# Scores of several heads in one PSUM bank, with one maximum and one mask, in a two-block transformer kernel

## The chip, the cores and the metric

The kernel runs on one core of one Trainium2 chip. Its metric is device time in microseconds for one execution, median of the runs. TensorE (PE) multiplies matrices into PSUM, whose eight banks hold 512 fp32 columns each; VectorE (DVE), ScalarE (ACT) and GpSimd (POOL) work element by element, GpSimd on SBUF alone; SyncE (SP) issues the DMA transfers. Each engine takes its instructions in the order in which they were laid down and waits on semaphores of the others.

## The reference

512 tokens of width 1024 pass two blocks in fp32: a gated linear attention layer, a sparse attention layer (four key heads with four query heads each, head width 64) and two hybrid layers (differential attention with four heads of two score maps each, beside stick-breaking attention with eight heads), each followed by a feed-forward network. What the change touches are two softmaxes.

In the sparse layer, with 512 tokens, all eight key blocks are selected, so the selected and the windowed attention are both plain causal softmaxes over the same queries:

```python
p_sel = masked_softmax(jnp.einsum('bkgqd,bkqmd->bkgqm', qc, ks) * scale, kpos <= qpos[:, None])
p_win = masked_softmax(jnp.einsum('bkgqd,bknd->bkgqn', qc, kw) * scale, win_mask)
o = gates[0] * o_cmp + gates[1] * o_sel + gates[2] * o_win
```

In the hybrid layers the weights are a difference of two softmaxes:

```python
sc = jnp.einsum('bhqd,bhkd->bhqk', qb, k).astype(jnp.float32) * scale
sc = jnp.where(mask, sc, -jnp.inf)
w = probs(qb1, k1) - lam * probs(qb2, k2)
```

## The kernel before, in words

Every fp32 value that goes into a large matmul is split into a high part of reduced precision (fp32r) and the rest, and a product is three matmuls (`mm3`, lines 321 to 323: high by high, low by high, high by low). Weights come as tiles of 128x1024 from memory, are split on ACT (L197) and DVE (L198), and feed the projections. These projections are most of PE's work.

The sparse layer (`nsa`) goes by head groups kh = 0 to 3 (one key head, four query heads), query blocks t of 128 tokens, and j = 0 (selected) or 1 (windowed): 32 units (kh, t, j). Groups 0 to 2 go through t = 0, 1, 2, 3, the last through 3, 2, 1, 0. A unit has two halves. `weights` takes, for each of four heads, n = (t+1)*128 columns of scores: two matmuls (L852, L853; keys high and low, the stacked query `qst` as the stationary operand) and a third that adds the causal mask from a bf16 identity and a 128x128 mask to the diagonal block (L854), all into a PSUM bank of the tag `pa`, of which there are three. Then DVE takes the negated row maximum (L1057), ACT the exponential with the row sum (L1059) into a tile of the tag `pe` (12 of them); after the four heads DVE makes the factors (reciprocal L1061, gate L1063) and scales the first head (L1069), POOL the three others (L1066). `values` transposes the weights on PE (L867, four heads' 128x128 blocks into one bank `pt`), splits them (ACT L870, DVE L871) and multiplies by the values into `po` (L1085, L1086); for j = 0 the compressed attention's weights go first (`ce`, L1079, L1080). `pipeline` calls `weights` of a unit ahead of `values` of the unit before.

The differential attention (`dweights1`, `dvalues`) does the same for four heads hd and two score maps c, with scores by `pair_scores` (L841 to L843), maximum L1275, exponential L1277, then reciprocal (L1279), the factor lambda (L1280), ACT's scaling of the second map (L1281) and DVE's combination (L1282). `dprep` prepares the next head's queries and keys: a rotation on POOL with a swapped copy by DMA, casts on ACT (L812, L824) and rests on DVE (L813, L825). The stick-breaking attention (`sweights1`) uses `pair_scores` too.

The order on each engine is not written out by hand: a scheduler of the tile framework lays all instructions down from its own estimate of times, tile by tile, with the buffer counts as limits. Functions of `fill` and `held` give it projections to lay between the units.

Of the kernel before, what the change touches and what calls it, by code (L numbers as in the profile page):

```python
# [17 lines left out]
AF = mybir.ActivationFunctionType  # L18
OP = mybir.AluOpType
AX = mybir.AxisListType  # L20

P = 128
# [75 lines left out]
class Kern:  # L98
# [10 lines left out]
    def setup(self, dram):  # L109
# [37 lines left out]
        for t, n in zip(bf, ("ident", "caus", "strict")):  # L147
# [7 lines left out]
                qst=8, sth=2, stl=2, q2h=2, q2l=2, k2h=4, k2l=4, pe=12, pth=4, ptl=4, otmp=1, on=4, onh=6, onl=6,  # L155
# [676 lines left out]
            out.append((k, lo))  # L832
        return out

    def pair_scores(self, q, k, t, mask):

        nc = self.nc
        n = (t + 1) * P
        ps = self.psum("pa")
        ts = slice(t * P, n)  # L840
        nc.tensor.matmul(ps[:, :n], q[:, ts], k[0][:, :n], start=True, stop=False)  # L841
        nc.tensor.matmul(ps[:, :n], q[:, ts], k[1][:, :n], start=False, stop=False)
        nc.tensor.matmul(ps[:, ts], self.identb, mask, start=False, stop=True)  # L843
        return ps[:, :n]

    def scores(self, q, k, t, mask):

        nc = self.nc
        n = (t + 1) * P
        ps = self.psum("pa")  # L850
        ts = slice(t * P, n)
        nc.tensor.matmul(ps[:, :n], q[:, ts], k[0][:, :n], start=True, stop=False)  # L852
        nc.tensor.matmul(ps[:, :n], q[:, ts], k[1][:, :n], start=False, stop=False)  # L853
        self.mask_mm = nc.tensor.matmul(ps[:, ts], self.identb, mask, start=False, stop=True)  # L854
        return ps[:, :n]

    def small(self, name, n, bufs=4, dt=F):
        if n > 16:
# [51 lines left out]
    def nsa(self, x):  # L910
        nc = self.nc
# [16 lines left out]
        for nb in range(2):  # L928
            nc.tensor.matmul(pk[:, :W], w2[:, nb * P:(nb + 1) * P], hid[:, nb * W:(nb + 1) * W],
                             start=nb == 0, stop=nb == 1)  # L930
# [38 lines left out]
        ps = self.psum("pd")  # L969
# [21 lines left out]
        def queries(kh, n):  # L991

            q = self.raw_block("nsa_w_in", 0, h, (2 * kh + n) * P, 0.125, "qs")
            st["q", kh, n] = q, self.stack_q(self.rope(q, tabs, eng=nc.vector))
# [42 lines left out]
        def weights(kh, t, j):  # L1037
            u = order[kh].index(t) * 2 + j
            if u == 0:
                if kh == 0:  # L1040
                    queries(0, 0)
                    queries(0, 1)
                    head_group(0)
                if kh < 3:
                    fill[:0] = [partial(queries, kh + 1, 0), partial(queries, kh + 1, 1), partial(head_group, kh + 1)]
            for i in range(pieces[kh][u]):
                if fill:
                    fill.pop(0)()
            qst, kd, o, e4 = st[kh]
            n = (t + 1) * P  # L1050
            sm = self.small("ss", 4)
            ps4 = []
            for g in range(4):
                sc = self.scores(qst[g], kd[j], t, self.causb)
                st["last"] = self.mask_mm
                mx = self.small("sm", 1, 8)
                nc.vector.tensor_reduce(mx, sc, axis=AX.X, op=OP.max, negate=True)  # L1057
                e = self.g("pe")
                nc.scalar.activation(e[:, :n], sc, AF.Exp, bias=mx, accum_out=sm[:, g:g + 1])  # L1059
                ps4.append(e)  # L1060
            nc.vector.reciprocal(sm, sm)  # L1061
            c = (j + 1) * 16 + kh * 4
            nc.vector.tensor_tensor(sm, sm, gate[:, t, c:c + 4], op=OP.mult)  # L1063
            for g in range(4):
                if g:
                    nc.gpsimd.tensor_scalar(ps4[g][:, :n], ps4[g][:, :n], sm[:, g:g + 1], 1.0,  # L1066
                                            op0=OP.mult, op1=OP.mult)
                else:
                    nc.vector.tensor_scalar(ps4[g][:, :n], ps4[g][:, :n], sm[:, g:g + 1], None, op0=OP.mult)  # L1069
            return ps4  # L1070

        def values(kh, t, j, ps4):
            qst, kd, o, e4 = st[kh]
# [36 lines left out]
        def out(n, ks, held=False):  # L1110
# [6 lines left out]
            nc.vector.tensor_tensor(xs[n], ps, xs[n], op=OP.add)  # L1117

        self.pipeline([(kh, t, j) for kh in range(4) for t in order[kh] for j in range(2)], weights, values)
        while fill:  # L1120
            fill.pop(0)()
# [62 lines left out]
    def hyb(self, x, layer, first):  # L1184
        nc = self.nc
# [4 lines left out]
        if first:  # L1190
# [9 lines left out]
            ps = self.psum("pt")  # L1200
            self.tok_sums(self.sqsum(x, gs), ps)
            a = self.sp.tile([P, 4], F, tag="ms", name="ms", bufs=3)
# [26 lines left out]
        for t, ps in enumerate(self.proj_wide(W, layer, h, (1024, 1280))):  # L1229
            sc = ycol[:, t:t + 1]  # L1230
# [23 lines left out]
        def dweights(hd):  # L1254
            if hd == 0:
                dprep(0)
            es = self.blocks("pe")
            ws = [dweights1(hd, 0, es[0])]
            if hd < 3:
                dprep(hd + 1)  # L1260
            for t in range(1, 4):
                ws.append(dweights1(hd, t, es[t]))
                if t == 2 and hd > 1:
                    svals(hd - 2)
            return ws

        def dweights1(hd, t, e0):
            q, k = st[hd]
            n = (t + 1) * P
            sm = self.small("ds", 2)  # L1270
            es = []
            for c in range(2):
                sc = self.pair_scores(q[c], k[c], t, self.causb)
                mx = self.small("sm", 1, 8)
                nc.vector.tensor_reduce(mx, sc, axis=AX.X, op=OP.max, negate=True)  # L1275
                e = self.g("pe")[:, :n] if c else e0
                nc.scalar.activation(e, sc, AF.Exp, bias=mx, accum_out=sm[:, c:c + 1])  # L1277
                es.append(e)
            nc.vector.reciprocal(sm, sm)  # L1279
            nc.vector.tensor_tensor(sm[:, 1:2], sm[:, 1:2], self.lam[:, layer:layer + 1], op=OP.mult)  # L1280
            nc.scalar.activation(es[1], es[1], AF.Copy, scale=sm[:, 1:2])  # L1281
            nc.vector.scalar_tensor_tensor(es[0], es[0], sm[:, 0:1], es[1], op0=OP.mult, op1=OP.subtract)  # L1282
            return es[0]
# [36 lines left out]
        def sweights(pr, a):  # L1320
            if a == 0 and pr == 0:
                sprep(0)
            rs = self.blocks("sbr")
            ws = [sweights1(pr, a, 0, rs[0])]
            if a == 0 and pr < 3:
                sprep(pr + 1)
            return ws + [sweights1(pr, a, t, rs[t]) for t in range(1, 4)]

        def sweights1(pr, a, t, r):
            q, k, o = st["s", pr]  # L1330
            n = (t + 1) * P
            z = self.pair_scores(q[a], k[a], t, self.strictb)
            l = self.g("sbl")[:, :n]
            nc.scalar.activation(l, z, AF.Abs)
            nc.scalar.activation(l, l, AF.Exp, scale=-1.0)
            nc.scalar.activation(l, l, AF.Ln, bias=1.0)
            nc.vector.scalar_tensor_tensor(l, z, 0.0, l, op0=OP.max, op1=OP.add)
            nc.vector.tensor_tensor_scan(r[:, ::-1], self.ones.to_broadcast([P, n]), l[:, ::-1], 0.0,
                                         op0=OP.mult, op1=OP.add)
            nc.vector.tensor_tensor(r, z, r, op=OP.subtract)  # L1340
            st["exp"] = nc.scalar.activation(r, r, AF.Exp)
            return r
# [22 lines left out]
        for n in range(16):  # L1365
            ps = self.proj(W, layer, h, 3072 + n * P)
            t = self.g("gate")
            nc.vector.tensor_tensor(t, ps, rbc, op=OP.mult)  # L1368
            gt.append(t)
        for n in range(16):  # L1370
            ins = nc.scalar.activation(gt[n], gt[n], AF.Sigmoid, bias=self.v("b_gate_2", layer, n))
            self.after(ins, last_exp)
        mh, ml = [], []
        for n in range(KB):
# [5 lines left out]
            a, b = self.split(gt[n], "mm")  # L1380
            mh.append(a)
            ml.append(b)
        for n in range(KB):
            ps = self.proj("w_out_2", layer, (mh, ml), n * P)
# [93 lines left out]
```

## Time and profile before

| | |
|---|---|
| median of 3 runs | 2833.21 us (2833.19 to 2834.01) |
| the profiled execution | 2835.08 us, of which the span of the trace is 2833.1 us |
| mean granted clock of TensorE | 0.991 |
| busy PE, DVE, ACT, POOL | 2773.4, 2019.9, 1366.3, 614.2 us |
| instructions | 39540, of them 14760 matmul records on PE |

The busy share is a mean over stages. The sparse layer's attention lies from 736 to 950 us, the differential attention from 1393 us in the first and from 2140 us in the second hybrid layer. Matmuls are pipelined: a matmul's duration in the trace is longer than its slot, and its cost to the stream is read from the starts of neighbours. A matmul in full fp32 has two records.

### The profile page before, as it was taken

What the parts mean: (1) busy time and instruction counts of PE and PEld (TensorE: products, weight loads), DVE (VectorE), ACT (ScalarE), POOL (GpSimd) and SP (SyncE); (2) the same over time, 40 slices, a digit from 0 to 9 for tenths busy, and PEclk for the clock granted to TensorE, in tenths of its full rate; (3) what the DMA queues carried; (4) which work ended last, traced back from release to release, by engine and by line L of the source; (5) the groups of instructions that cost most, each with busy time, mean ns of one, the idle gap of its engine ahead of it and who ended that gap; (6) DMA issues with size and microseconds to landing.
All of it is one profiled execution on the core that took longest, in us unless ns stands there. A gap on an engine that the chain in (4) does not pass through costs nothing.

```text
span 2833.1 us, 39540 instructions
## 1 busy us (share of the span) xinstructions
PE 2773.4 (98%) x14760; PEld 2355.9 (83%) x14760; DVE 2019.9 (71%) x3212; ACT 1366.3 (48%) x2474; POOL 614.2 (22%) x512
## 2 busy tenths in 40 slices
PE   8999999999999999999999998999999999999998
PEld 6888888888777788888788887899988878889997
DVE  7666755744698875575689768688848885687786
ACT  4444433433487543344477734344436775444333
POOL 4600000000542100000500003466423000056551
PEclk9999999999999999999999999999999999999999
DMA  4212333334520133332422223233313222423231
GB/s 184 75 55 93 98 97 97 97 96 140 148 71 31 45 94 98 97 98 90 129 81 67 86 78 115 86 114 103 126 50 101 75 65 87 140 82 98 88 110 49
DMA packets 102127, 264.58 MB, mean 93 GB/s; under 512 B 13472, under 2 KB 17184, under 8 KB 101936
## 3 DMA queue, kind: packets, MB, share of 16 engines
q1 hardware_dynamic: 101936, 262.07, 29.8%
q8 instruction: 116, 1.90, 0.3%
q14 instruction: 75, 0.61, 0.1%
HBM read 237.93 MB, written 2.10 MB: 85 GB/s over the span
## 4 chain that ended last, share of the span: by engine, by line
PE 88%; DVE 5%; ACT 3%; issue 2%; POOL 1%; DMA 1%; SPq 0%; DVEq 0%; ACTq 0%; POOLq 0%
PE pd L321 20%; PE pd L322 20%; PE pd L323 20%; PE q L323 4%; PE q L321 4%; PE q L322 4%; PE pt L867 2%; PE q L370 1%; PE q L371 1%; PE q L369 1%; PE pa L664 1%; PE pa L852 1%; PE po L1085 1%; PE po L1086 1%; PE pa L853 1%
## 5 line engine op out<-in xcount | busy, mean ns | idle before, releaser
L321 PE MATMUL pd<-hh,wh 128*128 128x512 f32 x1520 | 604.6, 398 | 5.0 <-DVE gate L1368 3.6
L322 PE MATMUL pd<-hl,wh 128*128 128x512 f32 x1520 | 600.3, 395 | 0.0
L323 PE MATMUL pd<-hh,wl 128*128 128x512 f32 x1520 | 599.2, 394 | 0.0
L197 ACT CAST wh<-wr 128x1024 fp32r<-128x1024 f32 x309 | 324.4, 1051 | 432.9 <-PE pd L322 316.7
L198 DVE TENSOR_TENSOR wl<-wr,wh 128x1024 fp32r<-128x1024 f32 x309 | 384.4, 1244 | 143.8 <-ACT wh L197 138.5
L377 DVE TENSOR_TENSOR xl<-yr,xh 128x512 fp32r<-128x512 f32 x322 | 323.7, 1016 | 40.1 <-ACT xh L376 39.9
L321 PEld LDWEIGHTS pd<-hh,wh 128*128 128x128 f32 x1520 | 288.9, 190 | 65.5 <-DVE gate L1368 4.1
L323 PEld LDWEIGHTS pd<-hh,wl 128*128 128x128 f32 x1520 | 288.3, 190 | 59.2 <-issue 0.5
L322 PEld LDWEIGHTS pd<-hl,wh 128*128 128x128 f32 x1520 | 288.6, 190 | 57.6 <-issue 0.2
L323 PE MATMUL q<-bbh,xl 128*128 128x256 f32 x952 | 269.7, 283 | 4.2 <-DVE xl L377 4.2
L321 PE MATMUL q<-bbh,xh 128*128 128x256 f32 x952 | 269.5, 283 | 0.0
L322 PE MATMUL q<-bbl,xh 128*128 128x256 f32 x952 | 269.3, 283 | 0.0
L376 ACT CAST xh<-yr 128x512 fp32r<-128x512 f32 x356 | 202.6, 617 | 115.6 <-POOL yr L248 40.1
L754 POOL TENSOR_TENSOR rcos<-al,rbc 128x512 f32<-128x512 f32 x3 | 4.2, 1401 | 929.0 <-ACT rbc L433 929.0
L323 PEld LDWEIGHTS q<-bbh,xl 128*128 128x128 f32 x952 | 182.7, 192 | 5.2 <-DVE xl L377 4.4
L322 PEld LDWEIGHTS q<-bbl,xh 128*128 128x128 f32 x952 | 182.6, 192 | 1.1
L321 PEld LDWEIGHTS q<-bbh,xh 128*128 128x128 f32 x952 | 182.8, 192 | 0.8
L535 DVE TENSOR_TENSOR x<-pd,x 128x512 f32<-128x512 f32 x84 | 57.5, 689 | 150.0 <-PE pd L323 149.8
L273 POOL TENSOR_TENSOR tb<-hn 128x256 f32<-128x256 f32 x8 | 8.1, 1015 | 636.6 <-DVE hn L471 634.5
L322 PE MATMUL pd<-ffl,wh 128*128 128x512 f32 x352 | 136.9, 389 | 0.0
L323 PE MATMUL pd<-ffh,wl 128*128 128x512 f32 x352 | 136.9, 389 | 0.0
L321 PE MATMUL pd<-ffh,wh 128*128 128x512 f32 x352 | 136.3, 389 | 0.0
(402 smaller groups left out, 6156.6 us busy)
## 6 DMA issues: line engine op xcount, KB each, us to landing
wr<-wp SPq DMA_DIRECT2D x309, 512.0 KB, 3.6
yr<-ws SPq DMA_DIRECT2D x136, 256.0 KB, 2.9
yr<-wp SPq DMA_DIRECT2D x118, 256.0 KB, 3.2
sw<-blk SPq DMA_DIRECT2D x80, 64.0 KB, 2.0
x<-xT SPq DMA_DIRECT2D x8, 256.0 KB, 5.8
yr<-cmp_k SPq DMA_DIRECT2D x4, 512.0 KB, 6.2
yr<-cmp_v SPq DMA_DIRECT2D x4, 512.0 KB, 6.4
sw<-qs SPq DMA_DIRECT2D x32, 64.0 KB, 2.0
```

What stands on the lines that cost most here:

```text
L197: nc.scalar.copy(hi, raw)
L198: nc.vector.tensor_tensor(lo, raw, hi.bitcast(F), op=OP.subtract)
L321: ins = mm(ps, wh, xh, start=first, stop=False)
L322: mm(ps, wh, xl, start=False, stop=False)
L323: mm(ps, wl, xh, start=False, stop=last)
L369: mm(ps, hh[k][:, tk], wh, start=k == 0, stop=False)
L370: mm(ps, hh[k][:, tk], wl, start=False, stop=False)
L371: mm(ps, hl[k][:, tk], wh, start=False, stop=k == KB - 1)
L376: self.nc.scalar.copy(hi, x)
L377: (eng or self.nc.vector).tensor_tensor(lo, x, hi.bitcast(F), op=OP.subtract)
L535: nc.vector.tensor_tensor(x[n], ps, x[n], op=OP.add)
L867: nc.tensor.transpose(pt[:n, i * P:(i + 1) * P], x, self.ident)
```

## The change

`pair_scores` goes, and `scores` takes lists of queries and keys: all of their scores lie side by side in one bank, the first matmul opens the bank, and one mask matmul with a broadcast mask closes it for all. `maxima` takes the row maxima of all heads in the bank in one reduction. In the sparse layer a bank holds 4, 2, 1, 1 heads at t = 0, 1, 2, 3; the weights of two heads lie in one tile at t = 0 and 1, and are scaled by one product of two inputs, the first pair on DVE and the second on POOL. In the differential attention a bank holds both maps at t = 0 and 1. The stick-breaking attention calls `scores` with one head.

```diff
-    def pair_scores(self, q, k, t, mask):
...
+    def scores(self, qs, ks, t, mask):
 
         nc = self.nc
         n = (t + 1) * P
-        ps = self.psum("pa")
+        ps = self.psum("pa")[:, :len(qs) * n].rearrange("p (g n) -> p g n", g=len(qs))
         ts = slice(t * P, n)
...
-        self.mask_mm = nc.tensor.matmul(ps[:, ts], self.identb, mask, start=False, stop=True)
-        return ps[:, :n]
+        for i, (q, k) in enumerate(zip(qs, ks)):
+            ins = nc.tensor.matmul(ps[:, i], q[:, ts], k[0][:, :n], start=i == 0, stop=False)
+            if i:
+                self.after(ins, opens)
+            else:
+                opens = ins
+            nc.tensor.matmul(ps[:, i], q[:, ts], k[1][:, :n], start=False, stop=False)
+        self.mask_mm = nc.tensor.matmul(ps[:, :, ts], self.identb,
+                                        mask[:, None, :].to_broadcast([P, len(qs), P]), start=False, stop=True)
+        return ps
+
+    def maxima(self, ps, name):
+
+        g = ps.shape[1]
+        mx = self.small(f"{name}{g}", g, 8)
+        self.nc.vector.tensor_reduce(mx, ps, axis=AX.X, op=OP.max, negate=True)
+        return mx
...
-            for g in range(4):
-                sc = self.scores(qst[g], kd[j], t, self.causb)
+            nb, nt = (4, 2, 1, 1)[t], (2, 2, 1, 1)[t]
+            for g in range(0, 4, nb):
+                sc = self.scores(qst[g:g + nb], [kd[j]] * nb, t, self.causb)
                 st["last"] = self.mask_mm
...
+                mx = self.maxima(sc, "sm")
+                for i in range(nb):
+                    if (g + i) % nt == 0:
+                        e = self.g("pe")[:, :nt * n].rearrange("p (g n) -> p g n", g=nt)
+                        ps4.append(e)
+                    nc.scalar.activation(e[:, (g + i) % nt], sc[:, i], AF.Exp, bias=mx[:, i:i + 1],
+                                         accum_out=sm[:, g + i:g + i + 1])
...
+            for i, e in enumerate(ps4):
+                w = sm[:, i * nt:(i + 1) * nt]
+                if nt > 1:
+                    (nc.gpsimd if i else nc.vector).tensor_tensor(e, e, w[:, :, None].to_broadcast([P, nt, n]),
+                                                                  op=OP.mult)
+                elif i:
+                    nc.gpsimd.tensor_scalar(e[:, 0], e[:, 0], w, 1.0, op0=OP.mult, op1=OP.mult)
                 else:
...
+                    nc.vector.tensor_scalar(e[:, 0], e[:, 0], w, None, op0=OP.mult)
+            return [e[:, i] for e in ps4 for i in range(nt)]
...
-            for c in range(2):
-                sc = self.pair_scores(q[c], k[c], t, self.causb)
...
+            nb = 2 if t < 2 else 1
+            for c0 in range(0, 2, nb):
+                sc = self.scores(q[c0:c0 + nb], k[c0:c0 + nb], t, self.causb)
+                mx = self.maxima(sc, "sm")
...
-            z = self.pair_scores(q[a], k[a], t, self.strictb)
+            z = self.scores([q[a]], [k[a]], t, self.strictb)[:, 0]
```

The scheduler lays the three stages down anew. The order up to the first scores of the sparse layer is the same. Two places follow. The first is PE at the first unit of t = 1 of the last head group (`pa` the score bank, `kdh` and `kdl` the keys, `al` the tile that holds the mask's identity, `pe` weights to be transposed, `ce` those of the compressed attention). Before:

```order
L867 MATMUL pt<-al,pe 128x128 x4
L852 MATMUL pa<-kdh,qst 128x256
L853 MATMUL pa<-kdl,qst 128x256
L854 LDWEIGHTS al
L854 MATMUL pa<-al 128x128
L867 MATMUL pt<-al,pe 128x128 x4
L852 MATMUL pa<-kdh,qst 128x256
L853 MATMUL pa<-kdl,qst 128x256
L854 LDWEIGHTS al
L854 MATMUL pa<-al 128x128
L852 MATMUL pa<-kdh,qst 128x256
L853 MATMUL pa<-kdl,qst 128x256
```

And the same place after (L842 and L847 are the two score matmuls, L848 the mask, L869 the transposes, L1094 and L1095 the values):

```order
L869 MATMUL pt<-al,pe 128x128 x4
L842 MATMUL pa<-kdh,qst 128x256
L847 MATMUL pa<-kdl,qst 128x256
L842 MATMUL pa<-kdh,qst 128x256
L847 MATMUL pa<-kdl,qst 128x256
L848 LDWEIGHTS al
L848 MATMUL pa<-al 128x2x128
L1095 MATMUL po<-ptl,vt 128x512
L1094 MATMUL po<-pth,vt 128x512
L869 MATMUL pt<-al,ce 31x128 x4
L842 MATMUL pa<-kdh,qst 128x256
L847 MATMUL pa<-kdl,qst 128x256
```

Two heads now share a bank and a mask, and value matmuls and transposes of the unit before stand between one bank and the next.

The second place is DVE in the first hybrid layer, from the first maxima of the differential attention to the first combined weights (`k2l` rests of the next head's keys, `ds` sums and factors, `sm` maxima, `wl` rests of a weight tile). Before:

```order
L1275 TENSOR_REDUCE sm<-pa 128x1 x3
L198 TENSOR_TENSOR wl<-wr,wh 128x1024
L825 TENSOR_TENSOR k2l<-rt,k2h 64x512 x2
L1279 RECIPROCAL ds<-ds 128x2
L1280 TENSOR_TENSOR ds<-ds,lam 128x1
L1282 SCALAR_TENSOR_TENSOR pe<-pe,ds 128x128
L1275 TENSOR_REDUCE sm<-pa 128x1
```

And the same place after (L856 is the maximum, L1290, L1291 and L1293 reciprocal, factor and combination):

```order
L856 TENSOR_REDUCE sm_11499<-pa 128x1
L198 TENSOR_TENSOR wl<-wr,wh 128x1024
L856 TENSOR_REDUCE sm_11433<-pa 128x2
L825 TENSOR_TENSOR k2l<-rt,k2h 64x512
L856 TENSOR_REDUCE sm_11485<-pa 128x2
L825 TENSOR_TENSOR k2l<-rt,k2h 64x512
L1290 RECIPROCAL ds<-ds 128x2
L1291 TENSOR_TENSOR ds<-ds,lam 128x1
L1290 RECIPROCAL ds<-ds 128x2
L1291 TENSOR_TENSOR ds<-ds,lam 128x1
L1293 SCALAR_TENSOR_TENSOR pe<-pe,ds 128x128
L1293 SCALAR_TENSOR_TENSOR pe<-pe,ds 128x256
```

The maximum of t = 1 for both maps moved between the two rests, and two reciprocals and factors stand ahead of the first combination.

## Rows read from the trace of the kernel before

**Rows 1.** The page's busy time of each engine, share of the span, instructions

```profile
PE 2773.4 (98%) x14760; PEld 2355.9 (83%) x14760; DVE 2019.9 (71%) x3212; ACT 1366.3 (48%) x2474; POOL 614.2 (22%) x512
```

**Rows 2.** Busy time by stretch: length, engines (instructions), PE's granted clock, DMA share, GB/s

```profile
736.70:743.50 6.80, 6.80 (x28) 6.11 (x28) 4.77 (x12) 2.08 (x8) 1.68 (x3) 0.53 0.59 140
780.00:860.00 80.00, 75.69 (x468) 56.79 (x467) 76.00 (x186) 65.49 (x183) 37.02 (x59) 1.00 0.25 62
```

**Rows 3.** PE's waits, whole span: total us, times, longest

```profile
PE pa L852 <- ACT pe L1059: 2.9, 6, 0.8
...
PE pt L867 <- DVE pe L1282: 2.6, 2, 2.2
...
PE pa L841 <- ACT pe L1277: 1.5, 3, 0.8
```

**Rows 4.** PE in order of time, scores of 128 columns: start, duration

```profile
937.28 0.31 PE L852 MATMUL pa<-kdh,qst 128*128 128x128 f32 x1
937.42 0.27 PE L853 MATMUL pa<-kdl,qst 128*128 128x128 f32 x1
937.54 0.23 PE L854 MATMUL pa<-al 128*128 128x128 bf16 x1
937.58 0.48 PE L1086 MATMUL po<-ptl,vt 128*128 128x512 f32 x1
```

**Rows 5.** PE in order of time, scores of 256 columns: [idle before, released by]

```profile
927.73 0.36 PE L852 MATMUL pa<-kdh,qst 128*128 128x256 f32 x1
...
928.05 0.23 PE L854 MATMUL pa<-al 128*128 128x128 bf16 x1
929.12 0.39 PE L852 MATMUL pa<-kdh,qst 128*128 128x256 f32 x1 [0.84 <-ACT pe L1059]
```

**Rows 6.** PE in order of time, first head of the differential attention

```profile
1400.41 0.39 PE L323 MATMUL pd<-hh,wl 128*128 128x512 f32 x1
1400.63 0.28 PE L841 MATMUL pa<-k2h,q2l 128*128 128x256 f32 x1
1400.75 0.28 PE L842 MATMUL pa<-k2l,q2l 128*128 128x256 f32 x1
...
1405.66 0.33 PE L867 MATMUL pt<-al,pe 128*128 128x128 f32 x1 [2.17 <-DVE pe L1282]
```

**Rows 7.** Groups of 700 to 960 us: busy us, mean ns, idle before, releasers

```profile
L1057 DVE TENSOR_REDUCE sm<-pa 128x1 f32<-128x512 f32 x32 | 21.7, 682 | 0.7 <-PE pa L854 0.4
...
L1066 POOL TENSOR_SCALAR pe<-pe,ss 128x256 f32<-128x256 f32 x24 | 13.0, 556 | 21.5 <-DVE ss L1063 14.8 <-PE pd L322 2.4 <-PE pt L867 2.3
L1057 DVE TENSOR_REDUCE sm<-pa 128x1 f32<-128x256 f32 x32 | 12.8, 411 | 2.6 <-PE pa L854 2.5
...
L1059 ACT ACTIVATE pe<-pa,sm 128x128 f32<-128x128 f32 x32 | 11.8, 375 | 5.6 <-DVE sm L1057 4.5 <-DVE ss L1061 0.8
L852 PE MATMUL pa<-kdh,qst 128*128 128x256 f32 x32 | 11.0, 344 | 1.5 <-ACT pe L1059 1.4
...
L1057 DVE TENSOR_REDUCE sm<-pa 128x1 f32<-128x128 f32 x32 | 8.9, 284 | 9.4 <-PE pa L854 9.1
...
L852 PE MATMUL pa<-kdh,qst 128*128 128x128 f32 x32 | 8.4, 275 | 1.0 <-ACT pe L1059 1.0
...
L1034 POOL TENSOR_TENSOR ce<-ce,cs 128x496 f32<-128x496 f32 x4 | 4.1, 1018 | 0.0
...
L1069 DVE TENSOR_SCALAR pe<-pe,ss 128x256 f32<-128x256 f32 x8 | 3.1, 381 | 0.1
...
L1023 DVE TENSOR_TENSOR ce<-ce,cm 128x496 f32<-128x496 f32 x4 | 2.8, 702 | 0.0
...
L1069 DVE TENSOR_SCALAR pe<-pe,ss 128x128 f32<-128x128 f32 x8 | 2.3, 288 | 0.2
```

**Rows 8.** DVE in order of time, up to the first combined weights

```profile
1400.28 2.82 DVE L825 TENSOR_TENSOR k2l<-rt,k2h 64x512 fp32r<-64x512 f32 x2 [1.83 <-ACT k2h L824]
...
1404.78 0.82 DVE L1282 SCALAR_TENSOR_TENSOR pe<-pe,ds 128x128 f32<-128x128 f32 x1 [0.53 <-ACT pe L1281]
```

More of the change, by code (lines that the diff above doesn't have):

```diff
@@ L833, in pair_k @@
         return out
-    def pair_scores(self, q, k, t, mask):
+    def scores(self, qs, ks, t, mask):
         nc = self.nc
         n = (t + 1) * P
-        ps = self.psum("pa")
+        ps = self.psum("pa")[:, :len(qs) * n].rearrange("p (g n) -> p g n", g=len(qs))
         ts = slice(t * P, n)
-        nc.tensor.matmul(ps[:, :n], q[:, ts], k[0][:, :n], start=True, stop=False)
-        nc.tensor.matmul(ps[:, :n], q[:, ts], k[1][:, :n], start=False, stop=False)
-        nc.tensor.matmul(ps[:, ts], self.identb, mask, start=False, stop=True)
-        return ps[:, :n]
[L846 to L853, printed above, removed]
-        self.mask_mm = nc.tensor.matmul(ps[:, ts], self.identb, mask, start=False, stop=True)
-        return ps[:, :n]
+        for i, (q, k) in enumerate(zip(qs, ks)):
[13 more added lines that the diff above has]
+        return mx
     def small(self, name, n, bufs=4, dt=F):
@@ L1052, in weights @@
             ps4 = []
-            for g in range(4):
-                sc = self.scores(qst[g], kd[j], t, self.causb)
+            nb, nt = (4, 2, 1, 1)[t], (2, 2, 1, 1)[t]
+            for g in range(0, 4, nb):
+                sc = self.scores(qst[g:g + nb], [kd[j]] * nb, t, self.causb)
                 st["last"] = self.mask_mm
[L1056 to L1060, printed above, removed]
+                mx = self.maxima(sc, "sm")
[5 more added lines that the diff above has]
+                                         accum_out=sm[:, g + i:g + i + 1])
             nc.vector.reciprocal(sm, sm)
@@ L1063, in weights @@
             nc.vector.tensor_tensor(sm, sm, gate[:, t, c:c + 4], op=OP.mult)
[L1064 to L1067, printed above, removed]
-                else:
-                    nc.vector.tensor_scalar(ps4[g][:, :n], ps4[g][:, :n], sm[:, g:g + 1], None, op0=OP.mult)
-            return ps4
+            for i, e in enumerate(ps4):
[5 more added lines that the diff above has]
+                    nc.gpsimd.tensor_scalar(e[:, 0], e[:, 0], w, 1.0, op0=OP.mult, op1=OP.mult)
+                else:
+                    nc.vector.tensor_scalar(e[:, 0], e[:, 0], w, None, op0=OP.mult)
+            return [e[:, i] for e in ps4 for i in range(nt)]
         def values(kh, t, j, ps4):
@@ L1271, in dweights1 @@
             es = []
-            for c in range(2):
-                sc = self.pair_scores(q[c], k[c], t, self.causb)
[L1274 to L1278, printed above, removed]
+            nb = 2 if t < 2 else 1
+            for c0 in range(0, 2, nb):
+                sc = self.scores(q[c0:c0 + nb], k[c0:c0 + nb], t, self.causb)
+                mx = self.maxima(sc, "sm")
+                for i in range(nb):
+                    c = c0 + i
+                    e = self.g("pe")[:, :n] if c else e0
+                    nc.scalar.activation(e, sc[:, i], AF.Exp, bias=mx[:, i:i + 1], accum_out=sm[:, c:c + 1])
+                    es.append(e)
             nc.vector.reciprocal(sm, sm)
```

## The prediction

> **What bounds the kernel now.** I read the busy times first: TensorE (PE) is busy 2773.4 us of the 2833.1 us span, 98% [rows 1]. So the time is PE's own stream of matmuls plus the few gaps in it, and work taken off VectorE (DVE), ScalarE (ACT) or GpSimd (POOL) counts only where PE waits for it. The change touches two places: the selected and windowed attention of the sparse mixer (736 to 950 us; 32 units of four heads, 8 for each query block t), and the differential attention of the two hybrid layers (from 1393 and from 2140 us; 32 pairs of scores, 8 for each t). Next I read busy time by stretch: from 780 to 860 us DVE is busy 76.0 us of 80 and PE 75.7 [rows 2]. There the two are nearly level, and a gain on PE alone would be taken back by DVE. Then I read what PE waits for [rows 3]. Waits for an exponential to free a bank of scores come to 2.9 us in the sparse mixer (L852) and 1.5 us in the hybrid layers (L841), and the first transposes of the differential stage wait 2.2 us for their weights (2.6 with a second, short wait). These, and the matmuls taken out, are all that the change can win back.
>
> **Mask matmuls.** Before, each of 192 score banks has its own mask. After, the sparse mixer has 1, 2, 4, 4 masks a unit at t = 0, 1, 2, 3 and the differential stage 1, 1, 2, 2 a pair: 8 x 11 + 8 x 6 = 136, so 56 go. But the columns stay: a wide mask writes 512 or 256 columns. What one costs is read from starts. A head of 128 columns takes 0.14 us to its second matmul, 0.12 to its mask and 0.04 from there to the next matmul, 0.30 in all [rows 4]; without a mask two such matmuls 0.12 apart take 0.24, so a mask is worth 0.06. A head of 256 columns takes 0.32 from its first matmul to its mask [rows 5] and 0.04 after it, 0.36; two matmuls of 256 columns run at 0.12 each [rows 6], so a second head without a mask in front takes 0.24, 0.12 less. Columns cost 0.22 - 0.12 = 0.10 us for 256 [rows 6], so 128 more in a mask cost 0.05. That gives 3 x 0.01 for each of 8 units at t = 0 of the sparse mixer, 0.07 for each of 24 joined pairs at t = 1 (16 there, 8 in the differential stage), and 0.01 for each of 8 pairs of the differential stage at t = 0: 0.2 + 1.7 + 0.1 = 2.0. The 0.12 in the first of these still holds back-to-back weight loads, which can hide a little further, so I take -2.4 us. Bounds: +0.5 (wide masks pay the full 0.22 of a 512-column matmul where four narrow ones paid 0.04 each, 8 times 0.06) and -3.9 (all 56 are worth 0.12, 6.7, less 56 x 0.05 for the columns).
>
> By the Trainium skill ("TensorE: Matmul & The Clock Gate", Back-to-back issue gap) a matmul's slot is its columns at the full clock and only some 2.5 ns beside. By that rule 56 masks fewer with the same columns save 0.1 us, not 2.4, and the sum below would come to 2830.4; the 0.30 against 0.24 of the rows speaks for more than the rule gives.
>
> **Maxima.** Four reductions of 0.284 us become one of 512 columns, 0.682 [rows 7]: 0.45 less for each of 8 units at t = 0. At t = 1 four of 0.411 become two of 0.682: 0.28 less. In the sparse mixer DVE loses 3.6 + 2.2 = 5.8 us, in the differential stage 8 x (0.568 - 0.411) + 8 x (0.822 - 0.682) = 2.4.
>
> **Weights of two heads in one tile.** On DVE the scaling of one head (0.288 at 128, 0.381 at 256 columns) becomes a product of twice the columns with a broadcast factor. No row shows that shape; the same kind on 496 columns takes 0.70 [rows 7], so 0.70 at t = 1, and between 0.35 and 0.70 at t = 0, of which I take 0.42. That is +0.13 and +0.32 for 8 units each, +3.6 us. DVE's net relief in the sparse mixer is 2.2 us, about half of it in the level stretch. On POOL three scalings of 0.556 at t = 1 become one product like that of 1.02 us (496 columns): 1.67 to 1.02, so the last weights are not later by this edit.
>
> **Banks.** Up to three banks take scores. A unit at t = 0 now fills one bank, not four, one at t = 1 two. Of the 2.9 us that PE waits in the sparse mixer for a bank, 1.0 stand in front of 128-column scores and 1.4 in front of 256-column ones [rows 7]; the clearest one is 0.84 us at t = 1, before the first head of a unit, whose bank an exponential of the unit before still holds [rows 5]. There the new order puts two heads and a mask into a bank, then transposes and value matmuls, so the three banks last for six heads. I take these 2.4 as gone, and half of the other 2.0 (wider scores, hybrid layers), which find banks free earlier: -3.4 us, bounds 0 and -4.4.
>
> **First transposes of the differential stage.** They wait 2.17 us until 1405.7 [rows 6], behind two key splits on DVE (2.8 us) and the reciprocal, the factor and the combination that follow [rows 8]. In the new order the wide maximum of t = 1 (0.68) stands between the two splits and two reciprocals and factors before the combination, so the weights come about when they did; but PE has the scores at t = 3 (two heads, some 1.2 us) ahead of that transpose instead of behind it. The work is the same, done in the gap. The next two transposes follow it sooner than before and can give part back: -0.7 us, bounds 0 and -1.8.
>
> **What is late next.** In the level stretch DVE is idle 4.0 us of 80, PE 4.3 [rows 2]. Where bank waits go there, PE comes sooner to transposes whose weights or whose split on DVE aren't ready. DVE gives about 1.1 us of relief there; I put what comes back at +1.4, bounds 0 and +2.9 (all of the mixer's bank waits).
>
> **Sum.** -2.4 - 3.4 - 0.7 + 1.4 = -5.1 us on the profiled execution's 2835.1 (span 2833.1 and 2.0 around it): 2830.0. That execution stands 1.9 above the median of the runs, 2833.2, so the forecast for the median is 2828.1. ACT's 2284 instructions are the same in kind and number. SP issues the same transfers; in the first third of the mixer the copies of the next queries and keys stand in another order among themselves and around two weight tiles, and no transfer stands among the waits of [rows 3], so I cost that at nothing; a copy that came late would hold the next head group's first scores, which have a unit of other scores in front of them.
>
> **Rivals.** *A larger gain.* All 4.4 us of bank waits and the 2.2 at 1405.7 go and nothing comes back: -2.4 - 4.4 - 2.2 = -9.0, 2824.2. A stretch at the lower clock could go with them: from 736.7 to 743.5 us the granted clock is 0.53 of full, the level of 1.2 GHz after PE had been thin, and costs 6.8 x 0.47 = 3.2 us [rows 2]; with one such less, 2821. For it: the banks are the commonest wait in these stages. Against: the order up to the first scores is unchanged, and so is what made that stretch.
>
> *No gain.* The columns are what a mask costs, and DVE, nearly full from 780 to 860 us, gives the rest back: -2 to +0.5 us, 2831 to 2834. For it: 76.0 of 80 [rows 2]. Against: the bank waits end on ACT, not on DVE.
>
> *Slower.* A unit's exponentials can only begin when the last of its heads has its mask and the wide maximum is through. At t = 0 the way from the last mask to the last exponential was 0.284 + 0.375 us; now it is 0.682 + 4 x 0.375 = 2.18 [rows 7], 1.5 longer, of which POOL's single product gives back about 0.6. If PE stands at the transposes each time, that is 8 x 0.9 in the mixer, and with 0.411 + 0.75 against 0.66, 8 x 0.5 in the differential stage: 11 us, with the masks' -2.4 net +9, 2842, and 2845 with one more fall of the clock. It decides from the point where PE's work between a unit's mask and its first transposes is shorter than that way with its factors and product, some 3.6 us. For it: the 2.17 us at 1405.7 are such a way laid bare. Against: behind the mask of the mixer's last unit at t = 0 stand 48 projection matmuls of 512 columns, 48 x 0.22 = 10.6 us, before its weights are transposed.
>
> By the Trainium skill ("GPSIMD Engine Reference", Engine selection) a product of two inputs takes POOL about twice as long as DVE, which would make it 1.4 us at t = 1 and lengthen this way by 0.4; the trace has 1.02 for 496 columns, which is less than the rule says.
>
> **How the numbers follow.** The forecast 0.49 (its own range 2826 to 2830.5), a larger gain 0.20, no gain 0.20, slower 0.11. A measurement of this kernel tells about 0.2%, 5.7 us, from no change: faster means under 2827.5, slower over 2838.9. Two fifths of the forecast's weight lie under 2827.5: 0.20 + 0.20 = 0.40 for faster. Of the slower case 0.09 lie over 2838.9. The rest, 0.51, is the same. The range leaves out the end of the larger gain and most of the slower case: 2820 to 2836.
>
> **What would show it.** In the changed profile: 56 matmuls fewer on PE; PE's waits for an exponential in front of scores under 1.5 us in all instead of 4.4; the wide maximum at about 0.68 us and DVE's product at 0.4 and 0.7; POOL's at 1.0 for 512 columns; the wait before the first transpose of the differential stage under 1.6 us; the stretches of the lower clock as many as before. Wrong it would be if PE's waits at transposes grew by more than 3 us, if a stretch at the lower clock came or went, or if the wide mask took much over 0.2 us.

## The result and the profile after

The changed kernel takes 2850.05 us (median of 4, 2846.53 to 2851.23) against 2833.2. The ratio of the runs is 1.0051, with an interval of 1.0039 to 1.0063; that is 14 us slower, and the two medians lie 16.9 us apart. The forecast was 2828.1 with a range up to 2836, so the sign was wrong.

The profiled execution is the fastest of the four (2846.5 us). Its page gives the engines, to be set beside [rows 1]:

```profile
PE 2775.9 (98%) x14704; PEld 2355.1 (83%) x14704; DVE 2028.7 (71%) x3156; ACT 1364.9 (48%) x2474; POOL 608.3 (21%) x480
```

The 56 matmuls are gone, and yet PE is busy 2.5 us longer. To see where, cut the span at PE's transposes of `ny` (L430), which open each norm; the last stretch ends at those of the final norm (L577). Busy time by stretch before: sparse mixer, feed-forward, first hybrid mixer, its feed-forward, second hybrid mixer, its feed-forward (length, then PE, PEld, DVE, ACT, POOL busy, PE's granted clock):

```profile
632.29:983.49 351.20, 338.67 (x1881) 270.48 (x1880) 269.03 (x533) 204.32 (x478) 112.29 (x146) 0.99 0.32 89
...
1354.49:1733.51 379.02, 370.97 (x1928) 310.46 (x1926) 291.36 (x522) 228.03 (x452) 39.66 (x26) 1.00 0.30 95
1733.51:2096.71 363.20, 358.98 (x2241) 326.27 (x2242) 276.82 (x391) 148.41 (x268) 171.53 (x118) 0.99 0.28 91
2096.71:2477.64 380.93, 372.04 (x1917) 310.95 (x1915) 283.46 (x498) 229.91 (x452) 39.77 (x26) 0.99 0.31 94
```

The same stretches after:

```profile
631.65:992.20 360.55, 342.77 (x1842) 271.96 (x1841) 274.67 (x493) 202.02 (x478) 109.19 (x114) 0.97 0.32 87
...
1364.07:1747.77 383.70, 371.64 (x1921) 310.40 (x1919) 293.08 (x514) 229.52 (x452) 39.58 (x26) 1.00 0.31 94
1747.77:2111.59 363.82, 359.16 (x2241) 325.82 (x2242) 275.40 (x391) 148.71 (x268) 171.50 (x118) 0.99 0.29 91
2111.59:2486.27 374.68, 369.05 (x1908) 309.01 (x1907) 283.67 (x490) 229.10 (x452) 40.14 (x26) 1.00 0.30 95
```

The sparse mixer is 9.3 us longer, and its clock fell from 0.99 to 0.97; the first hybrid mixer is 4.7 longer, the second 6.3 shorter. To compare stages across profiles, half of the time at the lower clock level is taken off below, which is what it costs where PE is busy throughout: an estimate, called "at full clock". So counted the sparse mixer takes 349.9 us instead of 347.0 (21.3 us at the lower level instead of 8.3), and 6.5 of the 9.3 us are clock. The last feed-forward, whose code is untouched, goes from 340.7 (2477.64 to 2818.30) to 343.7 us (2486.27 to 2829.96). PE's waits over the whole span, to be set beside [rows 3] (total us, times, longest):

```profile
PE q L323 <- DVE xl L377: 5.6, 2, 3.3
...
PE po L1095 <- DVE ptl L873: 2.7, 5, 0.9
...
PE pt L869 <- DVE pe L1293: 2.6, 3, 1.4
PE pa L842 <- ACT pe L1288: 2.5, 4, 0.9
...
PE pd L321 <- ACT onh L376: 2.2, 1, 2.2
PE pt L869 <- DVE ptl L873: 2.1, 5, 0.6
PE po L1088 <- DVE on L1102: 1.7, 3, 1.1
PE pa L842 <- ACT pe L1065: 1.7, 4, 0.6
```

The waits for a score bank come to 1.7 + 2.5 = 4.2 us, where they were 2.9 + 1.5 = 4.4: not gone, as forecast, but moved from the sparse mixer to the hybrid layers. Waits for splits (`ptl`) and sums (`on`) grew in the sparse mixer, and one for the last cast (`onh`) came. `onh` is the clearest. PE in order of time at the end of the sparse mixer:

```profile
934.92 0.39 PE L848 MATMUL pa<-al 128*128 128x512 bf16 x1
934.96 0.58 PE L321 MATMUL pd<-onh,wh 128*128 128x512 f32 x1
935.38 0.40 PE L322 MATMUL pd<-onl,wh 128*128 128x512 f32 x1
...
958.91 0.50 PE L1095 MATMUL po<-ptl,vt 128*128 128x512 f32 x1 [0.32 <-DVE ptl L873]
...
960.51 0.69 PE L1095 MATMUL po<-ptl,vt 128*128 128x512 f32 x1 [0.87 <-DVE ptl L873]
963.41 1.22 PE L321 MATMUL pd<-onh,wh 128*128 128x512 f32 x2 [2.20 <-ACT onh L376]
```

The last mask stands at 934.92; before it stood at 939.89, with bank waits of 1.3 us after 900 us. The mask releases the 48 held projection matmuls (`pd<-onh` from 934.96), and they are laid among the remaining transposes and values until 956. When the last values, sums and casts come, nothing is left to lay beside them, and PE stands bare. The clock falls there. Two stretches of the changed kernel, both at the 1.2 GHz level:

```profile
735.40:749.10 13.70, 13.70 (x44) 10.38 (x41) 8.78 (x18) 3.31 (x11) 7.52 (x9) 0.50 0.61 153
960.70:967.50 6.80, 4.60 (x11) 3.18 (x11) 2.13 (x4) 1.72 (x3) 0.00 (x0) 0.50 0.01 2
```

The second did not exist before. The first was 6.8 us long before [rows 2] and is twice that here.

### The profile page after: what moved, and what is told of

The parts are those of the page before. It is cut to its first block, busy times and chain, and to the rows that moved or that the text cites. A ratio compares the mean times of both kernels' runs of the same rounds, so it can differ in the third digit from the quotient of the medians.

```text
span 2844.7 us, 39308 instructions
## 1 busy us (share of the span) xinstructions
PE 2775.9 (98%) x14704; PEld 2355.1 (83%) x14704; DVE 2028.7 (71%) x3156; ACT 1364.9 (48%) x2474; POOL 608.3 (21%) x480
## 4 chain that ended last, share of the span: by engine, by line
PE 85%; DVE 8%; ACT 3%; issue 2%; POOL 1%; DMA 1%; SPq 0%; DVEq 0%; ACTq 0%; POOLq 0%
PE pd L321 19%; PE pd L322 19%; PE pd L323 19%; PE q L323 4%; PE q L321 4%; PE q L322 4%; PE pt L869 1%; PE q L371 1%; PE q L370 1%; PE q L369 1%; DVE ptl L873 1%; DVE bbl L264 1%; PE pa L842 1%; DVE sm L856 1%; PE pa L847 1%
```

## The experiments

Ratios are to the kernel before, run beside it on the same chip. "Clock" is the mean granted clock over all runs of a kernel: before has 0.990 beside the experiments, the changed kernel 0.9875, which is 7 us of span.

**One part at a time.** Four kernels set the number of heads in a bank (`nb`), of heads in a weight tile (`nt`) and of maps in a bank:

```diff
-            nb, nt = (4, 2, 1, 1)[t], (2, 2, 1, 1)[t]
+            nb, nt = NB[t], NT[t]      # e1: as changed; e2, e4: NB all 1; e2, e3: NT all 1
...
-            nb = 2 if t < 2 else 1
+            nb = ND[t]                 # e2: (2, 2, 1, 1); e1, e3, e4: all 1
```

> The whole change in the sparse layer (banks of 4 and 2 heads, weights of two heads in one tile), the differential attention as before. Theory A, the loss is made in the sparse layer (the changed kernel spends 9.3 us more there, 5.5 more in the first hybrid layer and 5.6 less in the second): 2841 to 2849 us, and the first hybrid layer as long as before. Theory B, the loss is the luck of a new order, whatever part is changed: anywhere from 2828 to 2849, with the hybrid layers of another length than before.

> The change in the differential attention alone, the sparse layer as before. Theory A: 2831 to 2835 us, as the first hybrid layer's +5.5 and the second's -5.6 cancel. Rival, the differential attention's wide maximum lengthens its way in both layers: 2838 to 2845.

> In the sparse layer banks, masks and maxima joined, but weights one head to a tile and scaled one by one as before; differential attention as before. Theory A1, the products of two heads on VectorE are the price (0.69 and 0.82 us where 0.29 and 0.38 stood, 8 times each, +6.7 us on an engine that is nearly full): without them VectorE has 5.8 us less to do, 2827 to 2832. Theory A2, the joined banks are the price (exponentials that begin only after the last head and the wide maximum): 2840 to 2847.

> In the sparse layer weights of two heads in one tile, scaled by one product, but a bank, a mask and a maximum for each head; differential attention as before. Theory A1 (the products are the price): VectorE has 6.7 us more to do and nothing less, 2838 to 2842. Theory A2 (the banks are the price): 2831 to 2835.

Measured: e1 1.0035 (1.0023 to 1.0048), e2 0.9989 (0.9980 to 0.9998), e3 1.0005 (0.9995 to 1.0014), e4 1.0032 (1.0019 to 1.0044). By these numbers theory A1, the products as the price, had won: tiles cost 0.3%, banks nothing (though the 2835.3 us of e3 lie in neither theory's range, and the 2842.8 of e4 just above A1's). The profile of e4 says otherwise. Its sparse mixer is only 3.8 us longer than before (632.7 to 987.6); 6.2 us come in the last feed-forward, 1500 us after the code that was edited. PE in order of time there:

```profile
2504.34 0.39 PE L323 MATMUL pd<-hh,xl 128*128 128x512 f32 x1
2505.15 0.39 PE L321 MATMUL q<-bbh,xh 128*128 128x256 f32 x1 [0.42 <-ACT xh L376]
2505.37 0.28 PE L322 MATMUL q<-bbl,xh 128*128 128x256 f32 x1
2509.06 0.58 PE L323 MATMUL q<-bbh,xl 128*128 128x256 f32 x1 [3.40 <-DVE xl L377]
2509.43 0.41 PE L321 MATMUL q<-bbh,xh 128*128 128x256 f32 x1
2509.65 0.63 PE L321 MATMUL pd<-hh,xh 128*128 128x512 f32 x1
```

Four matmuls of the first seven-product block (`q`) stand ahead of 96 projection matmuls (`pd`, 22 us of work), and wait 3.4 us for a split. The `pd` behind them runs at intervals of 0.43 us, half clock. In the kernel before these four stand behind the 96 in the second hybrid layer, but ahead of them in the first. PE's waits before have it:

```profile
PE q L323 <- DVE xl L377: 4.2, 1, 4.2
```

The scheduler, working from its own times, lays this place anew whenever something earlier shifts: in the changed kernel and e4 the four stand ahead in both layers, in e2 in the second alone, in e1 in the second and one of them in the first, in e3 as before. So e1, e2 and e4 had each been read with a place in it that they do not touch. Both hybrid feed-forward networks taken together, it adds 5.7 us to e4 against the kernel before, 0.6 to e1, and takes 2.9 from e2, where the wait of the first layer went as that of the second came. It is e4's reading that falls: at full clock its sparse mixer is 2.0 us longer than before, which is what is left for the tiles.

**The four matmuls put back.** A dependence without a semaphore, between two instructions of PE, keeps the block behind the last projection before it:

```diff
                 ins = self.mm3(ps, wh[:, ks], wl[:, ks], *x[r], k == 0, k == n - 1)
+                if k == 0:
+                    self.after(ins, self.proj_end)
```

In e5 this moves eight matmuls on PE against the changed kernel, in e6 four against the kernel before, and nothing on any other engine.

> The changed kernel with one thing put back: in the feed-forward networks of the two hybrid layers the first four matmuls of the first seven-product block (q, 128x256) are kept behind the 96 projection matmuls that they overtook. Nothing else moves on any engine. Theory C, part of the loss is this place, which the change does not touch: PE's waits for xl and xh there (3.3 + 0.6 us in the first layer, 2.2 in the second, and the half-clock stretch of 6.8 us at 1776 us) go, 5 to 9 us under the changed kernel, 2840 to 2846. Rival, the block only waits later: the same as the changed kernel within 2 us, 2847 to 2852.

> The kernel before with the same four matmuls kept behind the 96; only in the first hybrid layer does this move anything (they stood ahead there, with a wait of 4.2 us and 3.4 us at half clock). Theory C: 4 to 6 us less than before, 2827 to 2831. Rival, the block only waits later: no change, 2832 to 2836.

Measured: e5 1.0011 (1.0003 to 1.0020), e6 0.9978 (0.9969 to 0.9987). Theory C holds, at both kernels, and the rival falls: the wait does not come back later. The kernel before gains 6 us and the changed one 11, so this place is 5 of the 14 us. The first hybrid layer's feed-forward in e6, to be set beside its 363.20 us before:

```profile
1738.31:2095.04 356.73, 356.73 (x2241) 324.71 (x2242) 276.59 (x391) 148.16 (x268) 171.61 (x118) 0.99 0.29 93
```

PE is busy all of it. The 11 us (0.4%) of e5 are above the 5 to 9 expected; its mean clock rose from 0.9875 to 0.9894, 5 us of the 11.

**The bare tail.** Two kernels on e5 keep part of the held projections for the end of the sparse mixer. e7 keeps half of them (n over 3) back to the transposes of the compressed weights of the last query block; e11 a quarter (n over 5) to the last value matmul. On PE, e11 moves these 12 matmuls and one more against e5. The edit of e11:

```diff
-                    self.after(ins, st["last"])
+                    self.after(ins, st["tail"] if n > 5 else st["last"])
```

> The kernel of e5 with half of the 48 held projection matmuls of the sparse layer kept back until the compressed weights of its last query block are transposed. Theory D, joined banks let the last scores pass 5 us earlier, and the held projections are spent before the last block's outputs are through (waits of 0.3, 0.9 and 2.2 us at 959 to 963 us and a half-clock stretch of 6.8 us): 4 to 7 us under e5. Rival, the tail is as long as the way over transposes, values, sum and cast, whatever is laid there, or PE stands bare earlier: within 2 us of e5.

> The kernel of e5 with a quarter of the held projections of the sparse layer (12 of 48 matmuls, 2.7 us) kept back until its last value matmul. Keeping half of them back to an earlier point (e7) left the last wait of 2.3 us and the half-clock stretch behind it as they were, since they were spent by then. Theory D, the bare tail costs its wait and its stretch at half clock: the 2.2 us at the cast of the last output go, and the stretch of 6.8 us with it, 3 to 6 us under e5. Rival, what is kept back is missing before it, and the waits move there: within 2 us of e5.

Measured: e7 1.0010 (1.0001 to 1.0018), no gain; e11 0.9977 (0.9968 to 0.9986). In e7 the held matmuls are spent by 956.4, and the wait of 2.29 us for `onh` stands as it was: the place was chosen too early, so e7 tells nothing against theory D. In e11 PE's waits from 900 to 985 us are:

```profile
PE po L1098 <- DVE ptl L876: 1.3, 3, 0.6
PE pt L872 <- DVE pe L1081: 0.5, 1, 0.5
```

The wait for `onh` is gone, and its order shows what stands in its place:

```profile
956.23 0.50 PE L1098 MATMUL po<-ptl,vt 128*128 128x512 f32 x1 [0.62 <-DVE ptl L876]
956.57 0.40 PE L323 MATMUL pd<-onh,wh 128*128 128x512 f32 x1
956.80 0.40 PE L324 MATMUL pd<-onl,wh 128*128 128x512 f32 x1
```

The intervals behind it are 0.23 us, full clock, where after the bare tail they were 0.43. Theory D holds; its size, 9.6 us from e5 to e11 by the ratios, is over the 3 to 6 expected. At full clock the sparse mixer is 3.3 us shorter (350.5 to 347.2, the wait being 2.2 of it), and the mean clock rose from 0.9894 to 0.9910, some 4.5 us. The rest is not found; e5 and e11 ran on different chips, each beside the kernel before. That kernel has neither the wait for `onh` nor the stretch at half clock there, so it has no bare tail to cover.

**The products again.** e10 is e5 with one-head tiles, scaled one by one. e15 is e5 with both products on POOL:

```diff
-                    (nc.gpsimd if i else nc.vector).tensor_tensor(e, e, w[:, :, None].to_broadcast([P, nt, n]),
+                    nc.gpsimd.tensor_tensor(e, e, w[:, :, None].to_broadcast([P, nt, n]),
```

> The kernel of e5 with weights of one head to a tile, scaled one by one as before (one head on VectorE, three on GpSimd); joined banks, masks and maxima stay in both attentions. Theory A1, the products of two heads on VectorE are the price in the sparse layer: its stage goes from 360.5 to about 352.6 us as in the run with banks alone, so 5 to 9 us under e5, and with the differential attention's gain of about 4 us 2828 to 2834 us. Rival, the sparse stage's length is the luck of one order: within 3 us of e5.

> The kernel of e5 with both products of two heads on GpSimd, none on VectorE: 8 x (0.69 + 0.82) = 12 us less for VectorE in the sparse layer, 8 x (0.72 + 1.21) = 15 us more for GpSimd. Theory A1, VectorE's load in the level stretch is what the products cost: the sparse stage is 2 to 4 us shorter than in e5. Rival, it is how late the weights come that counts, whichever engine makes them (two products of 1.2 us one behind the other at t = 1): as long as in e5 or up to 4 us longer.

Measured: e10 0.9999 (0.9990 to 1.0008), e15 1.0019 (1.0010 to 1.0028), against 1.0011 for e5. DVE is busy 263.7 us in the sparse mixer of e15 and 275.1 in that of e5, and yet the mixer takes 363.4 us against 357.5 (351.3 against 350.5 at full clock). A1's forecast, 2 to 4 us shorter, fails: less load on VectorE alone does not shorten the mixer. e15's longest new waits are a split (2.0 us) and a sum (1.6) at 779 and 786 us, which fits the rival, late weights, without showing it alone. The intervals of e10 and e5 overlap (0.12% between them); the profiles say more, and follow below.

**What the two parts are worth, like for like.** e8 and e12 have the four matmuls put back and the sparse mixer as before; e20 and e14 also have the tail of e11. e12 sets `ND` to (2, 1, 1, 1). e14 joins banks in both attentions and keeps one-head tiles.

> The change in the differential attention alone (sparse layer as before), with the four matmuls kept behind the 96 as in e5 and e6, so like for like with e6. In the profiles so far the stage of this attention, less what half clock took, is 4 us longer than before in the first hybrid layer and 5 us shorter in the second. Theory E, the joined banks have no price or gain of their own there, the signs are the order's: within 3 us of e6, 0.997 to 0.999 of before. Rival, joined banks gain 2 to 4 us (fewer masks, no waits for banks) and the loss in the first layer is an accident: 0.9965 to 0.997.

> The kernel of e8 with both maps in one bank at t = 0 alone; at t = 1 a bank, a mask and a maximum for each map as before. If the 0.68 us maximum of t = 1 between the first weights' steps is what makes the first hybrid layer's stage 4 us longer, it is as long as before there, 2826 to 2830 us in all. Theory E (the signs are the order's): the two layers' stages differ from before by amounts of up to 5 us that follow no rule, with the sum within 4 us of e6.

> The whole change in the sparse layer, with 12 held matmuls kept for its tail (as in e11) and the four matmuls behind the 96 (as in e6); differential attention as before, PE's order after the sparse layer that of e6. Theory F, with the tail covered the sparse change is worth nothing: masks save 2 us, waits for weights and sums of the level stretch give it back, 2828 to 2832 us, 0.997 to 0.999 of before. Rival, the products keep a price of their own: 3 to 6 us over e6, 0.999 to 1.000.

> Joined banks, masks and maxima in both attentions, weights one head to a tile and scaled one by one, the tail covered and the four matmuls kept behind the 96. If the products cost about 3 us (e10 against e5) this is 3 us under e11: 0.996 to 0.997 of before, 2824 to 2829 us, and beats both kernels. If the products cost nothing once the tail is covered, it is as e11, 0.997 to 0.9985.

| kernel | ratio, interval | clock |
|---|---|---|
| before, four matmuls back (e6) | 0.9978, 0.9969 to 0.9987 | 0.9906 |
| sparse change, tail covered (e20) | 0.9978, 0.9969 to 0.9987 | 0.9905 |
| differential change (e8) | 0.9968, 0.9956 to 0.9980 | 0.9910 |
| differential change at t = 0 alone (e12) | 0.9969, 0.9959 to 0.9979 | 0.9910 |
| whole change, tail covered (e11) | 0.9977, 0.9968 to 0.9986 | 0.9910 |
| joined banks, one-head tiles, tail covered (e14) | 0.9965, 0.9953 to 0.9978 | 0.9912 |

Once PE's order is mended at the two places, the whole change (e11) is as fast as the kernel before with the one mend that it needs (e6), and so is its sparse part alone: theory F holds. The sparse mixer of e6, then of e20, shows how:

```profile
635.28:989.55 354.27, 341.75 (x1882) 272.72 (x1881) 270.19 (x533) 204.87 (x478) 111.97 (x146) 0.98 0.32 88
```

```profile
631.46:986.48 355.02, 340.41 (x1841) 270.40 (x1840) 273.65 (x493) 201.95 (x478) 108.58 (x114) 0.98 0.32 88
```

At nearly equal clock PE is busy 1.3 us less and idle 2.1 us more (14.6 against 12.5).

The differential part (e8) is 0.1% better than e6: its ratio falls in the range of the rival, a gain of joined banks, but its interval takes in theory E's too, so the total does not decide. The stages do. The first hybrid mixer of e8, then of e12 with a stretch inside it:

```profile
1357.25:1741.94 384.69, 372.73 (x1920) 311.55 (x1919) 294.07 (x514) 230.23 (x452) 38.74 (x26) 1.00 0.31 94
```

```profile
1356.52:1739.64 383.12, 372.85 (x1924) 312.78 (x1923) 291.51 (x518) 228.80 (x452) 39.46 (x26) 0.99 0.30 94
1417.30:1424.10 6.80, 6.02 (x28) 6.02 (x29) 5.74 (x13) 5.94 (x16) 3.11 (x2) 0.50 0.47 130
```

They look equally long, but e12's has 8.3 us at half clock and e8's 3.4. At full clock e12's takes 379.0 us and e8's 383.0, where the kernel before has 378.7. The second hybrid mixer takes 375.0 in e12, 373.6 in e8 and 378.9 before. All profiles agree: joined at t = 0 and 1 (nine kernels) the first takes 380.7 to 383.7 and the second 373.4 to 374.7, not joined (six kernels) 377.1 to 378.7 and 377.7 to 379.2. So the signs follow a rule, which theory E denied: the loss of 4 us in the first layer comes with the join at t = 1, as the first guess of e12 said, and most of the gain in the second with that at t = 0 (e12 is one profile). Whether the 0.68 us maximum itself makes the loss, or the order that the scheduler lays around it, is not shown.

The price of the products shows in the sparse mixers too. At full clock they are longer with products of two heads in all four pairs that differ in nothing else: by 1.8 us (e5 and e10), 1.2 (e11 and e14), 2.1 (e1 and e3) and 2.0 (e4 and before). Each is one profile; in whole times e14 and e11 differ by 0.12%, and their intervals overlap. e14, which joins banks without the products, has the shortest sparse mixer of all, 346.0. The best kernels, e14, e8 and e12, beat both kernels of the case; e14 takes 2826.72 us beside 2837.12 of the kernel before.

## Why the prediction was wrong, point by point

**Masks: right.** The profile after has the 56 matmuls less. PE in order of time, four heads of 128 columns with one mask:

```profile
752.42 0.28 PE L847 MATMUL pa<-kdl,qst 128*128 128x128 f32 x1
752.54 0.39 PE L848 MATMUL pa<-al 128*128 128x512 bf16 x1
752.58 0.58 PE L323 MATMUL pd<-hh,wl 128*128 128x512 f32 x1
753.00 0.40 PE L321 MATMUL pd<-hh,wh 128*128 128x512 f32 x1
```

And before, the last of the four narrow masks of the same unit:

```profile
752.80 0.24 PE L854 MATMUL pa<-al 128*128 128x128 bf16 x1
752.84 0.48 PE L321 MATMUL pd<-hh,wh 128*128 128x512 f32 x1
753.16 0.39 PE L322 MATMUL pd<-hl,wh 128*128 128x512 f32 x1
```

From the mask to the second start behind it are 0.46 us, where it took 0.36: the wide mask costs 0.10 more than a narrow one, under the 0.15 taken for its columns. The 1.3 us that PE is busy less in the sparse mixer of e20 than in that of e6 are near the 1.4 that the prediction's rows give for that mixer (0.2 at t = 0, 16 x 0.07 at t = 1). By the rule of the Trainium skill that the prediction names ("TensorE: Matmul & The Clock Gate", Back-to-back issue gap), which is given there for a matmul by itself, the estimate for the 40 masks fewer of that mixer is 0.1 us; the trace does not agree.

**Maxima right, products mis-sized.** Groups of DVE and POOL from 700 to 970 us, to be set beside [rows 7]:

```profile
L856 DVE TENSOR_REDUCE sm<-pa 128x2 f32<-128x512 f32 x16 | 10.8, 676 | 4.3 <-PE pa L848 4.2
...
L1073 DVE TENSOR_TENSOR pe<-pe,ss 128x512 f32<-128x512 f32 x8 | 6.6, 819 | 0.0
...
L1073 DVE TENSOR_TENSOR pe<-pe,ss 128x256 f32<-128x256 f32 x8 | 5.5, 686 | 0.1
...
L856 DVE TENSOR_REDUCE sm<-pa 128x4 f32<-128x512 f32 x8 | 5.4, 677 | 1.1 <-PE pa L848 1.1
...
L1073 POOL TENSOR_TENSOR pe<-pe,ss 128x512 f32<-128x512 f32 x8 | 9.7, 1207 | 11.2 <-DVE ss L1069 6.4 <-ACT pe L1065 2.4 <-ACT pth L872 1.8
```

At t = 0 and 1 the maxima save (8.9 + 12.8) - (5.4 + 10.8) = 5.5 us (5.8 forecast). The products take 5.5 + 6.6 = 12.1 where the scalings took 5.4, so +6.7 instead of +3.6: 0.69 and 0.82 us against the forecast's 0.42 and 0.70, POOL's 1.21 against 1.02. The forecast's durations are those of products that the other engine does not hold up (0.39 to 0.41 and 0.67 on DVE, 1.04 on POOL); left out was that the two engines do hold each other up (last section). DVE's relief of 2.2 us became 1.2 us more work. By the four pairs above that costs the mixer 1 to 2 us; by e15 it is not DVE's load alone.

**Bank waits: failed.** The term of -3.4 came to -0.2: the mixer's waits fell by 1.2, the hybrid layers' grew by 1.0. **First transposes: failed.** The wait for `pe` is 2.6 us in all as before, in three pieces (longest 1.4). Of the forecast's gains, -6.5 us with the masks' -2.4, none reached the total: with both places mended the change is worth nothing (0.9977 against 0.9978).

**What is late next: the step that failed most.** It gave back 1.4, bounds 0 and 2.9, and looked for it in the level stretch alone. From 770 to 870 us PE's waits for other things than a bank are 4.1 us after and 2.1 before, within those bounds. But the tail of the mixer and the feed-forward networks were put at nothing, without a row. In their place the runs show 9.6 us for the tail (e5 to e11) and 5 for the feed-forward networks (e5 and e6), which is about the whole loss. The prediction even named the 48 projection matmuls, as cover that speaks against the slow rival, from their place in the order before; the scores moved, and the same dependence that put them there used them up too early. And it took the order outside the two attentions for fixed. The `q` wait of 4.2 us in the waits of before was not read as a place that can turn.

**The slower rival** (2842 to 2845) was right in sign, 5 us short, and wrong in its mechanism: it placed the price at the transposes of every unit. **The clock** was held to be as before; the mean over the runs fell from 0.990 to 0.9875, which is about half of the 14 us. Two figures are off without effect: the page has 2474 ACT instructions before and after, not 2284, and the first maximum of the second hybrid layer stands at 2118 us, not 2140.

## What to carry to other kernels

Where a scheduler lays the order, compare the whole order of before and after on the engine that bounds, to the last instruction, and price each block that moved by what it waits for, also in code that the change does not touch. Before reading an ablation, see in its trace that it differs only in the stage that was edited: here e4 carried 5.7 us from a place 1500 us further on, more than the effect that it was built to show. And before setting one stage of two profiles side by side, take off what the clock cost in each: e8 and e12 looked alike and were 4 us apart. Filler work that is released by an event is gone earlier when the event comes earlier; tie the last of it to what it is meant to cover.

## What the hardware showed that was not expected

DVE's product of two heads takes 0.39 us for 256 columns while POOL is idle, and far more beside POOL. DVE, then POOL, in order of time, and DVE at a place without POOL:

```profile
756.62 1.48 DVE L1073 TENSOR_TENSOR pe<-pe,ss 128x256 f32<-128x256 f32 x1
```

```profile
756.52 1.29 POOL L766 TENSOR_TENSOR rt<-qs,rcos 128x512 f32<-128x512 f32 x1
757.77 0.80 POOL L1073 TENSOR_TENSOR pe<-pe,ss 128x256 f32<-128x256 f32 x1
```

```profile
807.76 0.39 DVE L1073 TENSOR_TENSOR pe<-pe,ss 128x256 f32<-128x256 f32 x1
```

The slow one ends at 758.10, some 0.3 us after POOL's product over `qs` ended at about 757.8: it seems to have stood until POOL was through. Of the eight, the four without POOL work beside them took 0.39 to 0.41 us, the two that POOL work covers wholly 1.48 and 1.50, and the two that it covers in part 0.47 and 0.42. By the Trainium skill ("SBUF — State Buffer", SBUF: two separate sides) a DVE operation with two SBUF inputs and a GpSimd operation that reads SBUF need one shared port pair: whichever starts first holds it for its whole instruction, and the other is blocked. The trace agrees, and the scalings that were replaced had one input.

The half-clock stretch at 735 us is twice as long in the changed kernel, though the order up to the first scores is the same: 13.7 us instead of 6.8, which is 3.4 us of time. It goes with the joined banks. Of the 13 profiles without another such stretch near 85 us, the eight with joined banks in the sparse layer have 13.7, and the five with a bank for each head 6.8. e3, e5 and e6 have a stretch near 85 us and then one of 3.4 (e3, at 723 us) or 6.8, joined or not: e5 shows 6.8 where the changed kernel, with the same instructions so far, shows 13.7. What makes the stretch longer is not shown. A single profile can thus differ by 3.4 us at one such place, and only the mean clock over many runs tells whether an edit lowers it.
